# Input projection of an encoder layer: q and k of the first half side by side, in units of seven products

## The chip, the cores and the metric

One core of a Trainium2 chip runs the kernel. The metric is device microseconds from start to end of one execution; several executions are timed and their median is given. Engines are named as in the profile: PE is TensorE (PEld its weight loads), DVE is VectorE, ACT is ScalarE, POOL is GpSimd, SP is SyncE, which here only issues DMAs.

## The reference

One encoder layer on 256 tokens of width 2048, in float32:

```python
hn = rms_norm(h, g_mix_pre)
q, k, v, xr, yg = split(hn @ w_in, [1024, 2048, 3072, 4096])   # w_in: 2048 x 5120
attn = neighborhood_attention(q, k, v, rpb)                    # 8 heads of 128
rec = rglru_bidirectional(xr, ...) * gelu(yg)
h = h + rms_norm(concat(rms_norm(attn), rms_norm(rec)) @ w_out, g_mix_post)
fn = rms_norm(h, g_ffn_pre)
h = h + rms_norm((silu(fn @ w_ffn_gate) * (fn @ w_ffn_up)) @ w_ffn_down, g_ffn_post)
gate = sigmoid(rms_norm(h, g_ple_pre) @ w_ple_gate)
h = h + rms_norm(gate * (p @ w_ple_proj), g_ple_post)
```

The change is in the line with `w_in`.

## The kernel before

**Split products.** Each float32 operand is split into a high and a low part: ACT casts the high part (`wh`, line 700), DVE subtracts it from the operand for the low part (`wl`, line 716). A product of a block of activations with a block of weights is three matmuls with 512 columns, high by high, low by high, high by low (line 758), all added up in one PSUM bank. The activations (`hT_hi`, `hT_lo`, lines 331 and 333) are made from the transposed input `xs` in 16 blocks of 128 rows; they are the weights that PE loads, and the columns of `w_in` stream past them.

**Chunks and tiles.** The 5120 columns of `w_in` are ten chunks of 512, worked through in `ORDER`: x0 v0 q0 k0 x1 q1 k1 v1 g0 g1. A chunk has two PSUM banks, one for each 128 tokens. A weight tile holds two blocks of 128 rows (a pair: 0, 2, ... 14) of one chunk, 512 KB; with its two blocks and two halves of tokens it feeds four products, 12 matmuls. x0 and v0 take turns, tile by tile, but for their last two tiles (`turns(first, hT, KS, apart=2)`); every later chunk runs its eight tiles one after the other. The first three tiles are loaded and split by halves. When a chunk is done, its post (`xr_post`, `v_post`, `qk_post`, `yg_post`) evacuates the banks with the scale `rstd_x`, which `norm_x` gets from the rows of x (`xn`, four loads), and goes on beside the next chunks: transposes, gates, scans, heads.

**Units of seven.** Later stages (feed-forward, the last projection) already take some pairs as units: two chunks side by side, the two blocks of a pair and the two halves of the tokens form a 2 x 2 by 2 x 2 product, which a scheme of the Strassen and Winograd kind does with seven products instead of eight. A `Group` places the steps of its units: `four` (four products with sums of weights and of activations, `four_products`), `two` and `one` (the other three). Between them `made_of_four` recombines the four banks, once for all units of a group. The sums of activations come from `sums_of`, those of weights from `sum_stream`, and the last one adds a block of the second tile by an accumulating DMA from POOL's queue (`added`). The units need the two chunks' tiles of a pair with two blocks swapped, which `SWAPPED` does when the arrays are laid out.

**Who sets the order.** A planner (`Plan`) places every instruction when the program is built: streams of work (`load_stream`, `hi_stream`, `lo_stream`, `make_hT`, the posts) offer their next operation with a cost, and it takes the one that by its own clock can start first. What it writes is one fixed order for each engine, which the hardware follows; semaphores make an instruction wait for what it needs, and what stands behind it on its engine waits too. Weight tiles have four buffers (`wr`), freed by the low part made from them, and the next load on SP waits for that. High and low parts have four buffers each, freed by PE.

## Time and profile before

| | before |
|---|---|
| median of 3 runs | 1138.61 us (1137.95 to 1138.9) |
| the profiled execution | 1138.81 us |
| its span, first to last instruction | 1137.0 us |
| mean granted clock of PE | 0.998 |
| PE busy | 1127.5 us, 99% of the span |
| DVE busy | 962.1 us, 85% |
| ACT busy | 741.0 us, 65% |
| POOL busy | 154.5 us, 14% |
| chain that ended last | PE 96%, DVE 1%, ACT 1%, DMA 1% |
| moved by DMA | 269.54 MB, mean 237 GB/s |

The busy time of PE counts matmuls that overlap each other in its pipeline, so a share of 99% is not 99% of its peak; whether PE had holes is read from its waits and from the distance between the starts of matmuls. The other engines' shares are means over stages with different loads, so a stage is looked at by itself.

### The profile page before, as it was taken

The page shows a single profiled execution, that of the slowest core. Times are in us where ns is not written, and L with a number is a line of the kernel's source. Part 1 is how long each engine was busy: PE and PEld are TensorE (multiplying, and loading weights), DVE is VectorE, ACT ScalarE, POOL GpSimd, SP SyncE. Part 2 cuts the span into 40 slices and gives each one's busy share as a digit, 9 for nine tenths or more (in the row PEclk, how much of TensorE's full clock was granted, in tenths as well). Part 3 has the DMA queues.
Part 4 walks back from the last instruction along what each step waited for, and adds up shares of the span by engine and source line. Part 5 has one row for each costly group of instructions (what it writes and reads, how often), then busy time and mean ns, then how long its engine had stood idle before and what let it go on. Part 6 is the DMA issues. An engine that isn't in the chain of part 4 may idle for free.

```text
span 1137.0 us, 15223 instructions
## 1 busy us (share of the span) xinstructions
PE 1127.5 (99%) x5140; PEld 938.2 (83%) x5140; DVE 962.1 (85%) x1250; ACT 741.0 (65%) x994; POOL 154.5 (14%) x245
## 2 busy tenths in 40 slices
PE   9999999999999999999999999999999999999997
PEld 8888888888888888888888888888888888888886
DVE  6768787788469998899998889999989988888986
ACT  6776788876448566566566656666565664676674
POOL 0000000000000032232011043132121223200200
PEclk9999999999999999999999999999999999999999
DMA  8867566565686986887887777897887788967862
GB/s 311 303 193 219 173 183 187 166 201 181 206 302 184 344 254 226 234 259 222 277 285 232 240 222 216 249 269 235 271 275 280 233 242 255 305 208 271 269 198 101
DMA packets 110686, 269.54 MB, mean 237 GB/s; under 512 B 36432, under 2 KB 42576, under 8 KB 109200
## 3 DMA queue, kind: packets, MB, share of 16 engines
q1 hardware_dynamic: 95568, 242.60, 64.0%
q0 software_dynamic: 14752, 25.84, 11.1%
q8 instruction: 40, 0.66, 0.2%
q14 instruction: 38, 0.31, 0.1%
q10 hardware_dynamic: 288, 0.14, 0.0%
HBM read 250.70 MB, written 9.44 MB: 229 GB/s over the span
## 4 chain that ended last, share of the span: by engine, by line
PE 96%; DVE 1%; ACT 1%; DMA 1%; issue 0%; SPq 0%; DVEq 0%; POOL 0%; ACTq 0%; POOLq 0%
PE acc L758 69%; PE acc L769 8%; PE acc L768 8%; PE acc L767 8%; PE tr L344 1%; DVE wl L716 0%; DMA sq<-ev 0%; PE half L2119 0%; PE acc L2119 0%; PE warm L2305 0%; PE pg L391 0%; PE pg L392 0%; PE pg L393 0%; ACT wh L700 0%; PE po L1435 0%
## 5 line engine op out<-in xcount | busy, mean ns | idle before, releaser
L716 DVE TENSOR_TENSOR wl<-wr,wh 128x1024 fp32r<-128x1024 f32 (+1 forms) x295 | 352.9, 1210 | 77.8 <-ACT wh L700 72.4
L700 ACT CAST wh<-wr 128x1024 fp32r<-128x1024 f32 (+1 forms) x295 | 304.9, 1042 | 136.8 <-PE acc L758 84.2
L758 PE MATMUL acc<-wh,hT_mix_hi 128*128 128x512 f32 x376 | 146.6, 390 | 0.0
L758 PE MATMUL acc<-wh,hT_mix_lo 128*128 128x512 f32 x376 | 146.3, 389 | 0.0
L758 PE MATMUL acc<-wl,hT_mix_hi 128*128 128x512 f32 x376 | 146.3, 389 | 0.0
L700 ACT CAST wh<-ple 128x1024 fp32r<-128x1024 f32 (+1 forms) x75 | 76.0, 1018 | 82.2 <-DVE ple L643 54.6
L363 POOL DMA_DIRECT2D mT<-mid x164 | 96.8, 636 | 238.3 <-DVE mid L353 117.6
L758 PE MATMUL acc<-wl,hT_hi 128*128 128x512 f32 x320 | 124.6, 390 | 0.0
L758 PE MATMUL acc<-wh,hT_hi 128*128 128x512 f32 x316 | 124.5, 394 | 0.0
L758 PE MATMUL acc<-wh,hT_lo 128*128 128x512 f32 x316 | 123.2, 390 | 0.0
L669 POOL DMA_DIRECT2D ple<-in_w_ffn_up x32 | 28.7, 897 | 539.7 <-DVE ple L643 386.3
L716 DVE TENSOR_TENSOR wl<-ple,wh 128x1024 fp32r<-128x1024 f32 (+1 forms) x75 | 88.0, 1177 | 9.3 <-ACT wh L700 9.3
L758 PEld LDWEIGHTS acc<-wl,hT_mix_hi 128*128 128x128 f32 x376 | 70.6, 188 | 14.7 <-DVE wl L716 0.2
L758 PEld LDWEIGHTS acc<-wh,hT_mix_hi 128*128 128x128 f32 x376 | 70.6, 188 | 14.6
L758 PEld LDWEIGHTS acc<-wh,hT_mix_lo 128*128 128x128 f32 x376 | 70.6, 188 | 14.6
L758 PEld LDWEIGHTS acc<-wl,hT_hi 128*128 128x128 f32 x320 | 60.1, 188 | 13.1 <-DVE wl L716 0.2
L758 PEld LDWEIGHTS acc<-wh,hT_lo 128*128 128x128 f32 x316 | 59.4, 188 | 11.6
L758 PEld LDWEIGHTS acc<-wh,hT_hi 128*128 128x128 f32 x316 | 59.4, 188 | 11.4
L758 PE MATMUL acc<-w,hT_mix_hi 128*128 128x512 f32 x144 | 47.3, 389 | 0.0
L716 DVE TENSOR_TENSOR wl<-lower,wh 128x1024 fp32r<-128x1024 f32 x35 | 42.4, 1215 | 3.1 <-ACT wh L700 3.1
L700 ACT CAST wh<-lower 128x1024 fp32r<-128x1024 f32 x35 | 36.6, 1052 | 10.7 <-PE acc L758 6.8
L758 PE MATMUL acc<-wh,hT_ffn_hi 128*128 128x512 f32 x96 | 37.8, 393 | 0.4 <-ACT hT_ffn_hi L331 0.4
(472 smaller groups left out, 2536.6 us busy)
## 6 DMA issues: line engine op xcount, KB each, us to landing
wr<-in_w_in SPq DMA_DIRECT2D x77, 512.0 KB, 4.5
wr<-in_w_ffn_gate SPq DMA_DIRECT2D x70, 512.0 KB, 5.6
wr<-in_w_ffn_down SPq DMA_DIRECT2D x54, 512.0 KB, 6.0
wr<-in_w_ffn_up SPq DMA_DIRECT2D x50, 512.0 KB, 5.0
wr<-in_w_out SPq DMA_DIRECT2D x32, 512.0 KB, 4.4
wr<-in_w_ple_gate SPq DMA_DIRECT2D x30, 512.0 KB, 4.7
lower<-in_w_ffn_up SPq DMA_DIRECT2D x27, 512.0 KB, 6.4
third<-in_w_ffn_gate SPq DMA_DIRECT2D x18, 512.0 KB, 5.7
```

Source lines behind the costliest of these rows:

```text
L344: nc.tensor.transpose(tr[:, b, t * P : (t + 1) * P], e[:, t, sl], ident)
L363: (nc.gpsimd if i in pool else nc.sync).dma_start(dst[32 * j : 32 * j + 32, :, :, i, :], src[32 * i : 32 * i + 32, :, :, j, :],)
L669: nc.gpsimd.dma_start(dst, src, accum_op=ALU.add)
L700: nc.scalar.copy(his[i][:, 0 : src.shape[1], :] if n == 2 else his[i][:, j, :], src)
L716: nc.vector.tensor_tensor(out=los[i][:, m, :], in0=src, in1=f32(his[i][:, m, :]), op=ALU.subtract)
L758: nc.tensor.matmul(accs[t], x[:, sl], w[:, j, :], start=st and m == 0, stop=sp and m == 2, **group)
L767: nc.tensor.matmul(dst, x[0], wh, start=start, stop=False, skip_group_check=seeded)
L768: nc.tensor.matmul(dst, x[1], wh, start=False, stop=False, skip_group_check=seeded)
L769: nc.tensor.matmul(dst, x[0], wl, start=False, stop=stop, skip_group_check=seeded)
```

## The change

The first half's q and k become a `Group` with two units, the pairs 0 and 2 (`IN_KS`). Their `four` steps stand among the tiles of x0 and v0, both behind the fifth pair of those (`IN_AT`); x0 and v0 therefore use the banks of the kind `sm`, so that q0 and k0 can have the other four (`acc`) meanwhile. Behind x0 and v0 come q0's and k0's other pairs: 4, then the first unit's `two`, 6, then the second unit's `two` and both `one`, and then the last four tiles of q0 and the last four of k0. The second tile of a unit goes to a place of its own (`in_rows`, memory that q and k use later), and so do the sums (`in_both`, `here`). The loads of the rows of x move behind the units' loads. The pool of this stage is opened at the start, and tiles that share memory with the new ones are opened when chunks end.

```diff
+IN_KS = (0, 2)
+IN_AT = (5, 5)
...
+    (lambda c: (("w_in", c), ("w_in", c + 2)), (0,), IN_KS),
...
     def load_stream():
...
+            if i in in_load:
+                for kb, f in extra_loads.get((i, 0), ()):
+                    yield dma(kb)
+                    f()
+                j, second = in_load[i]
+                yield dma(512, take=None if second else "wr")
+                loaded[i] = in_rows[j] if second else raw_tile(i)
+                nc.sync.dma_start(loaded[i], a[w][n0 // N, k // 2])
+                done(ev_load[i])
+                continue
...
+    def in_sum_stream():
+
+        for j, i in enumerate(into.own):
+            yield ev_load[i]
+            yield ev_load[i + 1]
+            Q, R, both = loaded.pop(i), loaded.pop(i + 1), in_both[j]
+            yield dve(3 * N)
+            nc.vector.tensor_tensor(out=both[:, 0, :], in0=Q[:, 0, :], in1=Q[:, 1, :], op=ALU.add)
+            nc.vector.tensor_tensor(out=both[:, 1, :], in0=both[:, 0, :], in1=R[:, 1, :], op=ALU.add)
+            nc.vector.tensor_tensor(out=Q[:, 1, :], in0=Q[:, 1, :], in1=R[:, 1, :], op=ALU.add)
...
+    def in_last_sum(j):
+        late, last = into.last[j][:2]
+        there = Event()
+        yield from added(in_both[j][:, 1, :], late[:, 0, :], there)
...
+    def in_sums():
+        more = t1["pool"].tile([P, 2, N], F32R, name="sums_more")
+        pairs = [[x.rearrange("p k s -> p (k s)") for x in at0], (more[:, 0, :], more[:, 1, :])]
+        for n, kx in enumerate(IN_KS):
...
+            yield from sums_of(hT, kx, *p, t1["here"])
...
     for i in range(2 * NT):
-        extra_loads.setdefault((10 + i, 0), []).append(load_xn(i))
+        extra_loads.setdefault((14 + i, 0), []).append(load_xn(i))
...
-        ch = Chunk(post(half), (open_p1, second_tiles)[n] if n < 2 else None)
-        if n < 2:
-            first.append((ch, "w_in", n0 + half * N))
+        ch = Chunk(post(half), {0: open_hs, 1: open_v, 2: open_qk, 3: second_tiles}.get(n), slot="sm" if n < 2 else "acc")
+        made_of[c] = ch, "w_in", n0 + half * N
         if n == 1:
-            turns(first, hT, KS, apart=2)
-        elif n > 1:
-            seg(ch, "w_in", n0 + half * N, hT, KS, after=start_biases if n == 3 else None)
+            first = [made_of[m] for m in ORDER.split()[:2]]
+        if n == 3:
+            into = Group([made_of[m] for m in ORDER.split()[2:4]], hT, KS, IN_KS, apart=4)
+            into.own, into.twos, into.last = [], {}, {}
+            m = len(KS) - 2
+            for i, k in enumerate(KS[:m]):
+                for j, b in enumerate(IN_AT):
+                    if i == b:
+                        into.four(j)
+                for d, w, o in first:
+                    seg(d, w, o, hT, [k], i == 0, False)
...
+            for d, w, o in first:
+                seg(d, w, o, hT, KS[m:], first=False)
+            steps = list(('0', '1ab'))
+            m = len(into.rest) - into.apart
+            for i in range(m):
+                into.pair(i)
...
+            for d, w, o in into.chunks if into.apart else ():
+                seg(d, w, o, hT, into.rest[m:], first=False)
+        elif n > 3:
+            seg(*made_of[c], hT, KS)
...
+    plan.add(in_sums(), late=-LATE)
+    plan.add(in_sum_stream(), late=-LATE)
```

DVE at the start of the program, before. `wl_153` is the low part of x0's first tile (made by halves), `wl_166` that of v0's first tile, `wl_200` that of x0's second one, `hT0_lo` a block of the activations' low part:

```order
L716 TENSOR_TENSOR wl_153<-wr_137,wh_152 128x512
L716 TENSOR_TENSOR wl_166<-wr_141,wh_165 128x512 x2
L333 SCALAR_TENSOR_TENSOR hT0_lo_80<-xs0_81,g_first_67,hT0_hi_79 128x256 x2
L716 TENSOR_TENSOR wl_200<-wr_145,wh_199 128x512 x2
L716 TENSOR_TENSOR wl_214<-wr_149,wh_213 128x1024
```

The same place now. `wl_186` is x0's first tile, `wl_200` v0's first one, `wl_228` x0's second one, `here` the sums of activations:

```order
L927 TENSOR_TENSOR here_146<-hT0_hi_79,hT0_lo_80 128x256
L766 TENSOR_TENSOR wl_186<-wr_170,wh_185 128x512
L927 TENSOR_TENSOR here_146<-hT0_hi_79,hT0_lo_80 128x256
L766 TENSOR_TENSOR wl_200<-wr_174,wh_199 128x512
L336 SCALAR_TENSOR_TENSOR hT0_lo_80<-xs0_81,g_first_67,hT0_hi_79 128x256 x2
L934 TENSOR_TENSOR here_146<-here_146 128x128
L766 TENSOR_TENSOR wl_200<-wr_174,wh_199 128x512
L934 TENSOR_TENSOR here_146<-here_146 128x128
L766 TENSOR_TENSOR wl_228<-wr_178,wh_227 128x512
```

The two blocks of `hT0_lo` and an addition stand ahead of the second half of v0's first tile now; they stood behind it.

DVE some 20 us later, before. `wl_300` and `wl_322` are x0's and v0's fifth tiles (pair 8), the two behind them the sixth ones:

```order
L716 TENSOR_TENSOR wl_300<-wr_272,wh_299 128x1024
L333 SCALAR_TENSOR_TENSOR hT0_lo_80<-xs1_82,g_first_67,hT0_hi_79 128x256 x4
L716 TENSOR_TENSOR wl_322<-wr_285,wh_321 128x1024
L716 TENSOR_TENSOR wl_357<-wr_318,wh_356 128x1024
L716 TENSOR_TENSOR wl_377<-wr_354,wh_376 128x1024
```

The same place now. `wl_348` and `wl_387` are x0's and v0's fifth tiles, `wr_356` and `rows_qh` the two tiles of the first unit, `wr_384` and `rows_ql` those of the second, `both` the sums of weights, from which `wl_420` is made:

```order
L336 SCALAR_TENSOR_TENSOR hT0_lo_80<-xs1_82,g_first_67,hT0_hi_79 128x256 x2
L766 TENSOR_TENSOR wl_348<-wr_306,wh_347 128x1024
L336 SCALAR_TENSOR_TENSOR hT0_lo_80<-xs1_82,g_first_67,hT0_hi_79 128x256 x2
L330 TENSOR_TENSOR sums_more_148<-here_146,sums_more_148 128x512
L673 TENSOR_TENSOR both_kl_143<-wr_356 128x512
L674 TENSOR_TENSOR both_kl_143<-both_kl_143,rows_qh_140 128x512
L675 TENSOR_TENSOR wr_356<-wr_356,rows_qh_140 128x512
L766 TENSOR_TENSOR wl_387<-wr_324,wh_386 128x1024
L673 TENSOR_TENSOR both_pp_144<-wr_384 128x512
L674 TENSOR_TENSOR both_pp_144<-both_pp_144,rows_ql_141 128x512
L675 TENSOR_TENSOR wr_384<-wr_384,rows_ql_141 128x512
L766 TENSOR_TENSOR wl_420<-both_kl_143,wh_419 128x1024
```

Between the low parts of x0's and v0's fifth tiles stand a split and three additions of weights now, two of which read the unit's second tile.

SP at the loads of this place, before (`wr_285` is v0's fifth tile, `xs1` the last blocks of the transposed input, `xn` the rows of x):

```order
L612 DMA wr_285<-in_w_in 128x1024
L957 DMA xs1_82<-in_xT 128x1024
L965 DMA xn0_83<-in_x 128x1024
L612 DMA wr_318<-in_w_in 128x1024
L965 DMA xn0_83<-in_x 128x1024
```

and now (`wr_324` is v0's fifth tile):

```order
L626 DMA wr_324<-in_w_in 128x1024
L1015 DMA xs1_82<-in_xT 128x1024
L591 DMA wr_356<-in_w_in 128x1024
L591 DMA rows_qh_140<-in_w_in 128x1024
L591 DMA wr_384<-in_w_in 128x1024
L591 DMA rows_ql_141<-in_w_in 128x1024
L1023 DMA xn0_83<-in_x 128x1024
```

The four tiles of the units are issued where the rows of x were; up to there SP's order is the one of before.

## Rows read from the trace of the kernel before

**Rows 1.** The cores' spans and granted clock.
```profile
core 0: 1137.0 us, clock 0.998
```

**Rows 2.** Waits of PE, whole span: us in total, times, longest us.
```profile
PE final L2206 <- ACT diag L2204: 2.5, 1, 2.5
PE warm L2305 <- POOL ones L309: 1.1, 1, 1.1
PE acc L758 <- ACT hT_ffn_hi L331: 0.4, 1, 0.4
PE sc L391 <- DVE pp L327: 0.3, 1, 0.3
```

**Rows 3.** Chain of waits, one long piece: start us, us, what.
```profile
264.35 81.62 PE acc L758 x360
```

**Rows 4.** By stretches: PE, PEld, DVE, ACT, POOL busy us, PEclk, DMA share, GB/s.
```profile
10.00:20.00 10.00, 10.00 (x46) 8.13 (x45) 8.26 (x12) 6.92 (x11) 0.00 (x0) 1.00 0.98 370
20.00:30.00 10.00, 10.00 (x46) 8.29 (x45) 6.93 (x12) 7.74 (x13) 0.00 (x0) 1.00 0.96 344
30.00:40.00 10.00, 10.00 (x46) 8.29 (x45) 5.23 (x7) 8.67 (x13) 0.00 (x0) 1.00 0.93 349
...
90.00:100.00 10.00, 10.00 (x46) 8.27 (x45) 9.86 (x18) 5.73 (x8) 0.00 (x0) 1.00 0.69 194
```

**Rows 5.** Groups by line and shape, low and high parts of weights: busy us, mean ns.
```profile
L716 DVE TENSOR_TENSOR wl<-wr,wh 128x1024 fp32r<-128x1024 f32 x289 | 348.9, 1220 | 76.3 <-ACT wh L700 71.2 <-DMA wr<-in_w_in 1.8 <-PE acc L758 1.8
...
L700 ACT CAST wh<-wr 128x1024 fp32r<-128x1024 f32 x289 | 301.2, 1051 | 135.4 <-PE acc L758 84.2 <-PE acc L768 9.5 <-DMA wr<-in_w_in 6.2
```

**Rows 6.** Timeline from 5 to 12.5 us: start us, us, instruction [idle before <-releaser].
```profile
5.57 0.63 PE L743 MATMUL acc<-wh,hT_lo 128*128 128x512 f32 x1
...
6.00 0.60 PE L742 MATMUL acc<-wh,hT_hi 128*128 128x512 f32 x1
...
6.64 2.37 DVE L716 TENSOR_TENSOR wl<-wr,wh 128x512 fp32r<-128x512 f32 x3 [0.89 <-ACT wh L700]
...
9.30 0.91 ACT L331 ACTIVATE hT_hi<-xs,g_first 128x256 fp32r<-128x256 f32 x2 [1.02 <-DMA xs<-in_xT]
...
9.84 0.89 DVE L333 SCALAR_TENSOR_TENSOR hT_lo<-xs,g_first,hT_hi 128x256 fp32r<-128x256 f32 x2 [0.83 <-ACT hT_hi L331]
...
10.32 0.39 PE L758 MATMUL acc<-wl,hT_hi 128*128 128x512 f32 x1
...
10.75 1.29 DVE L716 TENSOR_TENSOR wl<-wr,wh 128x512 fp32r<-128x512 f32 x2
...
11.50 0.19 PEld L758 LDWEIGHTS acc<-wl,hT_hi 128*128 128x128 f32 x1
11.69 0.39 PE L758 MATMUL acc<-wl,hT_hi 128*128 128x512 f32 x1
```

**Rows 7.** Timeline of DVE near 18 and 363 us: instructions in a row.
```profile
17.72 2.35 DVE L716 TENSOR_TENSOR wl<-wr,wh 128x1024 fp32r<-128x1024 f32 x2
...
363.20 0.76 DVE L869 TENSOR_TENSOR ple<-hT_mix_hi,hT_mix_lo 128x256 f32<-128x256 f32 x2
364.00 1.02 DVE L876 TENSOR_TENSOR ple<-ple 128x128 f32<-128x128 f32 x4
```

**Rows 8.** Timeline of DVE from 24 to 28 us, its two waits for hT_hi.
```profile
24.20 0.89 DVE L333 SCALAR_TENSOR_TENSOR hT_lo<-xs,g_first,hT_hi 128x256 fp32r<-128x256 f32 x2 [0.98 <-ACT hT_hi L331]
...
26.49 1.69 DVE L333 SCALAR_TENSOR_TENSOR hT_lo<-xs,g_first,hT_hi 128x256 fp32r<-128x256 f32 x4 [0.27 <-ACT hT_hi L331]
```

**Rows 9.** DMA issues of the first 60 us: count, KB each, median us to landing.
```profile
wr<-in_w_in SPq DMA_DIRECT2D x21, 512.0 KB, 5.5
xn<-in_x SPq DMA_DIRECT2D x4, 512.0 KB, 10.0
```

**Rows 10.** By stretches at the end of the run, columns as in rows 4.
```profile
1128.00:1130.00 2.00, 0.70 (x5) 0.30 (x3) 1.15 (x4) 1.67 (x2) 0.00 (x0) 1.00 0.42 164
1130.00:1132.00 2.00, 0.70 (x2) 0.30 (x2) 1.50 (x5) 0.97 (x5) 0.00 (x0) 1.00 0.00 0
```

More of the change, by code (lines that the diff above doesn't have):

```diff
@@ L494, in two @@
             self.twos[j] = i
-            lower[self.own[j] + 1] = -1
+            if self.lhs is not hT:
+                lower[self.own[j] + 1] = -1
             segs.append((two_products, self, j, i))
@@ L650, in sum_stream @@
             done(ev_raw[two, 2])
+    def in_sum_stream():
[7 more added lines that the diff above has]
+            nc.vector.tensor_tensor(out=Q[:, 1, :], in0=Q[:, 1, :], in1=R[:, 1, :], op=ALU.add)
+            raws[i] = both
+            done(ev_raw[i, 2])
+            raws[i + 1], raws[into.twos[j]] = Q, R
+            done(ev_raw[i + 1, 2])
+            done(ev_raw[into.twos[j], 2])
+    def in_last_sum(j):
+        late, last = into.last[j][:2]
+        there = Event()
+        yield from added(in_both[j][:, 1, :], late[:, 0, :], there)
+        yield there
+        raws[last] = in_both[j][:, 1:2, :]
+        done(ev_raw[last, 2])
+    def in_sums():
+        more = t1["pool"].tile([P, 2, N], F32R, name="sums_more")
+        pairs = [[x.rearrange("p k s -> p (k s)") for x in at0], (more[:, 0, :], more[:, 1, :])]
+        for n, kx in enumerate(IN_KS):
+            if n == 2:
+                for e in hT.ev[8:]:
+                    yield e
+                pair = big(1, "sums_in").rearrange("p (n m) s -> p n (m s)", m=2)
+                pairs.append((pair[:, 0, :], pair[:, 1, :]))
+            p = pairs[n]
+            yield from sums_of(hT, kx, *p, t1["here"])
     ends_with, ends_in = {}, {}
@@ L726, in lo_stream @@
                 plan.add(last_sum(i), plan.now, -2 * SOON)
+            if i in into.own:
+                plan.add(in_last_sum(into.own.index(i)), plan.now)
     MM = 0.2263
@@ L811, in second @@
             done(there)
-        yield ev_rf
-        yield act(N)
-        u, v = (t2["pool"].tile([P, N], F32, tag="junk", name="u", bufs=2) for _ in range(2))
+        if group.lhs is hT:
+            u, v = (t1["ig"][:, n, :, :].rearrange("p c s -> p (c s)") for n in range(2))
+            yield act(N)
+        else:
+            yield ev_rf
+            yield act(N)
+            u, v = (t2["pool"].tile([P, N], F32, tag="junk", name="u", bufs=2) for _ in range(2))
         nc.scalar.copy(u, q1)
@@ L850, in one_product, with sums_of @@
         spent(i)
-    def sums_of(lhs, kx, hi, lo):
+    def sums_of(lhs, kx, hi, lo, here=None):
         lhs.sums[kx] = {
@@ L859, in sums_of @@
         yield lhs.ev[kx + 1]
-        kind = "mid" if lhs is hP or kx == 6 else "T4"
+        kind = None if here is not None else "mid" if lhs is hP or kx == 6 else "T4"
         for j in range(2):
@@ L863, in sums_of @@
             yield dve(S, take=None if j else kind)
-            if not j and kind == "mid":
+            if not j and not kind:
+                e, f = here[:, 0, :], here[:, 1, :]
+            elif not j and kind == "mid":
                 at_ = mid_tile()
@@ L1077, in open_p1, with open_v, open_qk, open_hs @@
         nc.gpsimd.memset(ssr, 0.0)
+        in_rows.extend(p1.tile([P, 2, N], F32, tag=n, name=f"rows_{n}") for n in ("qh", "ql", "kh"))
+        in_both.extend(p1.tile([P, 2, N], F32, tag=n, name=f"both_{n}") for n in ("kl",))
+        in_both.append(
+            p1.tile([P, 4 * NT * KEYS], F32, tag="pp", name="both_pp")[:, 0 : 2 * N].rearrange("p (m n) -> p m n", m=2)
+        )
+        in_both.append(sq_tile().rearrange("p t k q -> p t (k q)"))
+        t1["here"] = p1.tile([P, 2, N], F32, tag="vh", name="here")
+    def open_v():
+        for n in ("vh", "vl"):
+            t1[n] = t1["pool"].tile([P, NT, N], F32R, tag=n, name=n)
+    def open_qk():
+        for n in ("qh", "ql", "kh", "kl"):
+            t1[n] = t1["pool"].tile([P, HB, S], F32R, tag=n, name=n)
+        t1["pp"] = t1["pool"].tile([P, 2, NT, 2, KEYS], F32R, tag="pp", name="pp")
+    def open_hs():
+        t1["hs"] = big(0, "hs", F32)
     def sq_tile():
@@ L1100, in second_tiles @@
         plan.reach(ev_x)
+        t1["rec_hi"] = big(1, "rec_hi")
         t1["rec_lo"], t1["attnT"] = big(2, "rec_lo"), big(3, "attnT", F32)
@@ L2259, in layer @@
         places.append(lower[i])
+    in_load = {i + n: (j, n) for j, i in enumerate(into.own) for n in range(2)}
+    for i in in_load:
+        ev_load[i] = Event()
+    for j, i in enumerate(into.own):
+        gives[i] = gives[into.twos[j]] = gives[into.last[j][1]] = "x"
     first_slot = {i: n % 2 for n, i in enumerate(sorted(fours))}
@@ L2288, in layer @@
     soonest = min(fours)
+    open_p1()
     plan.add(load_stream(), late=lambda: (
```

19 lines of the change are left out of this document (12 added, 7 removed).

## The prediction

> **What bounds the kernel now.** I read the span first [rows 1], then TensorE's waits [rows 2]. Over the whole run it waited four times: 1.1 us before the first warm-up matmul, 2.5 us before the last matmul, 0.4 and 0.3 us between. The chain of waits gives the rate of the rest [rows 3]: 360 matmuls in 81.62 us, 0.2267 us each. So TensorE issues without a hole from the first weights on, and the time can move in two ways only: by the count of matmuls, and by new holes.
>
> Whether holes come is read where the change works, in the first 50 us. By stretches of 10 us [rows 4], VectorE is busy 8.26, 6.93 and 5.23 us from 10 us on, ScalarE 6.92 to 8.67, the DMA engines 98, 96 and 93%. That is some 9.6 us of idle VectorE in 30 us, and what it gets in addition has to fit in there at the right places, since an engine takes its instructions in the order in which they stand.
>
> **What it removes.** In two units q0 and k0 take seven products instead of eight: 2 x 1 x 3 matmuls of 512 columns fewer. 6 x 0.2267 = **1.36 us gained**. Nothing hides TensorE, so this counts in full, and it is all that can be gained.
>
> **What it adds.** VectorE gets 4 additions of 256 columns and 8 of 128 for the sums of activations, 2 low parts of 512 for those, 6 additions of 512 for the weights, 3 more low parts of 1024 (a unit casts three tiles and a half instead of two) and 4 additions of 512 that recombine the banks. At 0.38 and 0.26 us for 256 and 128 columns [rows 7], 0.65 for 512 [rows 6] and 1.22 for 1024 [rows 5] that is 1.5 + 2.1 + 1.3 + 3.9 + 3.7 + 2.6 = 15.1 us; the first four kinds (8.8 us) fall before the units. It is not free, and steps 1 and 2 price it. ScalarE gets 3 casts of 1024 at 1.05 us [rows 5], 2 of 512 and 2 copies, some 5.5 us: nothing as long as VectorE, which gets three times as much, is later; if it were ScalarE, the price is a cast, 1.05 us. The two accumulating loads of 256 KB go on GpSimd's queue, empty in this stage, and what they bring is used behind q0's and k0's next pairs and x0's and v0's last ones, some 25 us later: nothing. The four loads of x rows, moved on SP's queue behind the units' loads, serve only the scale with which x0 is evacuated, and that too moves back by the units' 5.4 us: nothing, or what x0's post is late, and TensorE doesn't wait for that before its transposes. These take the banks that x0 and v0 now hold; they stood 186 matmuls into the stage and stand 210 in now, and the 24 are the units' own: nothing. In the later stages TensorE's order is the same and buffers only rotate: nothing, as TensorE waited 0.4 us there [rows 2].
>
> **Step 1, a hole at 10 us.** Here the order decides. Before, the low part of v0's first pair, second half, was the third of three that ended at 6.64 + 2.37 = 9.01 us, and TensorE used it at 10.32 us [rows 6], 1.3 us later. Now the low part of hT of blocks 2 and 3 and one addition of 128 columns stand **ahead** of it. That hT_lo waits for ScalarE's hT_hi, which waits for a load until 9.30 us, so it starts at 9.84 us [rows 6], and the change leaves this load and ScalarE's order up to it as they were. So 9.84 + 0.41 + 0.41 (the row of two: 0.89 less the last one's tail) + 0.24 (128 columns) = 10.9 us, and 0.69 us for the low part (1.29 for two): 11.59 us. From there to TensorE: the next low part ended at 11.44 us (10.75 + 0.69), the weight load that waited for it began at 11.50 and its matmul at 11.69 [rows 6], 0.25 us. So TensorE goes on at 11.84 instead of 10.32: **1.5 us lost**. Bounds: 1.25 if the passage costs nothing; 1.8 if each small addition costs a wait as well.
>
> Behind this hole TensorE is 1.5 us late. The next five low parts are late by the small additions among them, and fit into that.
>
> **Step 2, the units' supply.** Next I set VectorE's work against TensorE's need, up to the low part of v0's fifth pair (v0/8), which now stands behind three weight additions. From 11.5 us VectorE has 12 hT_lo at 0.41, 2 additions of 256 at 0.38, 7 of 128 at 0.25, 7 operations of 512 at 0.61 and 7 low parts of 1024 at 1.13 us (spacings from [rows 6, 7]): 4.9 + 0.8 + 1.7 + 4.3 + 7.9 = 19.6, done at 31.1 us if it never waits. Before, it waited in this stretch 0.98 and 0.27 us for hT_hi [rows 8], which hangs on loads that don't come earlier now. I take the same 1.25 us: 32.35 us. TensorE asks, 90 matmuls after the hole, at 10.32 + 1.5 + 20.4 - 0.25 = 32.0 us: 0.35 us late. Then 3 additions and one low part (2.95 us) stand against 12 matmuls (2.72): 0.2 more. After that a tile of the units needs 1.13 us and lasts 1.36. **0.55 us lost.**
> Bounds: nothing, if VectorE waits 0.6 us less. Above, the units' second tiles decide. The first one is issued when x0/6's low part is done, about 24.1 us (54 matmuls after the hole), half a microsecond behind the first tile, and its addition stands at about 30 us. A load of weights took 5.5 us here in the median, one of x rows 10.0 [rows 9]. With 5.5 it lands as VectorE comes to it; with 10.0 everything behind waits 4.1 us longer.
>
> **Sum.** The profiled execution took 1138.81 us (its span 1137.0), 0.20 above the median of 1138.61. 1138.81 - 1.36 + 1.5 + 0.55 = 1139.5, on the scale of the median 1139.3. I say **1139.3 us**: the hole at 10 us eats the gain, the units' supply costs a little more. A measurement of this kernel can tell about 0.2% (2.3 us) from no change, so this counts as none.
>
> **Rivals.**
> A. *No hole*, the full gain: 1138.61 - 1.36 = 1137.25 us. For it: the idle time in [rows 4] suffices for the added work in sum. Against: step 1 hangs on one load at 9.30 us and the order behind it, not on the sum; that load would have to land 1.5 us earlier. 0.07.
> B. *The second tiles land late*, on the side of slower. Behind the addition that waits for them stand the low part of v0/8 and all that the units need. 0.7 us are lost by the forecast already (1139.3 less 1138.61), so another 1.6 us make more than 0.2%: it decides once such a tile takes more than 7.1 us instead of 5.5. For it: DMA engines 93 to 98% busy, and the 10.0 us of the x rows. Against: those rows now come later, so less is queued in front. 1139.8 to 1143.4 us. 0.20, half of it beyond 0.2%.
> C. *TensorE's clock falls in the hole.* The matmuls at 5.57 and 6.00 us start 0.43 us apart [rows 6], 1.2 GHz by their rate against 0.2267 us at 2.4 GHz, and TensorE had been at work since about 1 us. Some 5.3 us at half rate again would cost 2.65 us: 1141.9, slower. Against: before its last matmul TensorE stood for 2.5 us [rows 2], and the granted clock read 1.00 in both stretches around that [rows 10]. 0.04. The Trainium skill (TensorE: Matmul & The Clock Gate, Why this matters for your kernels) warns that idle gaps between bursts of matmuls bring the clock back to half; by this rule a change that opens a gap pays more than the gap, and the trace shows no such fall after its one long gap.
> D. *q0's post falls into VectorE's fullest stretch.* q0 ends 10.9 us ahead of k0 instead of 21.8, so its turn and splits move towards those of k0 and the first heads, and VectorE was busy 9.86 of 10 us from 90 to 100 us [rows 4]. A low part or two that come late there cost 1.13 us each: 1140.4 to 1141.6 us. 0.08.
>
> **How the numbers follow.** The forecast case has 0.61 and runs from 1138.4 (step 1 at its lower bound less a little, step 2 nothing) to 1140.3. The range 1137.9 to 1141.2 leaves out A, the upper third of B, C and a little of D, 0.2 in all. Slower by over 0.2% (above 1140.9): half of B, C, a third of D, 0.16. Faster by over 0.2% (below 1136.3): no term reaches it, since 1.36 us is all there is; 0.02 for what I don't see. The same: 0.82.
>
> **What would show it.** Step 1: a wait of TensorE (or of its weight load) for VectorE's low part at 10.3 us, some 1.5 us long, that low part ending near 11.6 us behind hT_lo at 9.84. Step 2: waits of under 1 us in all between 24 and 36 us, the first before v0/8. Elsewhere 0.2267 us between matmuls and six matmuls fewer. VectorE waiting long for rows_qh or rows_ql would show B, matmuls 0.43 us apart after 12 us C, TensorE waiting between 70 and 110 us D. I am wrong if TensorE has no wait at 10 us, or if its new waits sum to over 4 us.

## The result, and the profile after

The changed kernel took **1144.12 us** (median of 4 runs, 1142.26 to 1145.45) beside 1138.58 us of the kernel before in the same session (1137.95 to 1138.90): ratio 1.0047, 95% interval [1.0033, 1.0062]. It is slower by 5.5 us. The forecast was 1139.3 us, its range ended at 1141.2, and "slower by over 0.2%" had 0.16. The profiled execution took 1143.78 us, its span 1142.0 instead of 1137.0 [rows 1]; the differences below are told on the span.

TensorE's waits in the kernel after, over the whole span (us in total, times, longest us), with the same columns as [rows 2]:

```profile
PE acc L810 <- DVE wl L766: 3.1, 2, 1.7
PE final L2307 <- ACT diag L2305: 2.5, 1, 2.5
PE warm L2414 <- POOL ones L312: 1.1, 1, 1.1
PE tr L347 <- ACT pr L1456: 1.0, 1, 1.0
PE tr L347 <- ACT ev L1186: 0.5, 1, 0.5
PE acc L810 <- ACT hT_ffn_hi L334: 0.4, 1, 0.4
PE acc L794 <- ACT wh L750: 0.3, 1, 0.3
```

The waits of 2.5, 1.1 and 0.4 us are those of before. New are two for low parts (3.1 us), two of transposes (1.5 us) and one of 0.3 at the start. They sit in two places, the first 40 us and around 154 to 187 us. The first place by stretches, columns as in [rows 4]:

```profile
10.00:20.00 10.00, 8.60 (x38) 6.81 (x37) 9.36 (x18) 7.88 (x13) 0.00 (x0) 1.00 0.87 315
20.00:30.00 10.00, 8.31 (x37) 6.50 (x36) 7.73 (x16) 6.47 (x12) 0.00 (x0) 1.00 0.83 292
30.00:40.00 10.00, 9.88 (x44) 7.73 (x43) 9.86 (x14) 6.17 (x9) 0.99 (x1) 1.00 0.98 366
```

TensorE is no longer full. VectorE went from 8.26 to 9.36 us in the first stretch, where work was added. What was not forecast stands in the last two columns: the DMA engines fell from 98 and 96% to 87 and 83%, and from 370 and 344 to 315 and 292 GB/s. They moved less although there was more to load.

**The hole at 10 us** in the timelines of VectorE and TensorE (start us, us, instruction, idle before and its releaser):

```profile
10.22 0.89 DVE L336 SCALAR_TENSOR_TENSOR hT_lo<-xs,g_first,hT_hi 128x256 fp32r<-128x256 f32 x2 [1.37 <-ACT hT_hi L334]
11.02 0.28 DVE L934 TENSOR_TENSOR here<-here 128x128 f32<-128x128 f32 x1
11.22 0.69 DVE L766 TENSOR_TENSOR wl<-wr,wh 128x512 fp32r<-128x512 f32 x1
...
10.16 0.40 PE L810 MATMUL acc<-wh,hT_lo 128*128 128x512 f32 x1
11.96 0.50 PE L810 MATMUL acc<-wl,hT_hi 128*128 128x512 f32 x1 [1.40 <-DVE wl L766]
```

This is step 1, term by term: the two hT_lo, the addition of 128 columns, the low part. From 10.16 to 11.96 us, less one matmul of 0.23, are 1.57 us lost; 1.5 were forecast. Two small misses nearly cancel in that: the low part was done at 11.91 us instead of 11.59, as the load came later, and TensorE went on 0.05 us behind it instead of 0.25.

**The hole at 24 us** was in no step:

```profile
23.31 1.69 DVE L336 SCALAR_TENSOR_TENSOR hT_lo<-xs,g_first,hT_hi 128x256 fp32r<-128x256 f32 x4 [1.99 <-ACT hT_hi L334]
24.91 1.22 DVE L766 TENSOR_TENSOR wl<-wr,wh 128x1024 fp32r<-128x1024 f32 x1
...
24.11 0.39 PE L810 MATMUL acc<-wh,hT_lo 128*128 128x512 f32 x1
26.18 0.50 PE L810 MATMUL acc<-wl,hT_hi 128*128 128x512 f32 x1 [1.69 <-DVE wl L766]
```

The low part at 24.91 us is x0/6's. In the kernel before it is the second of the two in the row at 17.72 us [rows 7], ahead of the hT_lo of blocks 8 to 11, which begin there at 22.35 us:

```profile
22.35 0.87 DVE L333 SCALAR_TENSOR_TENSOR hT_lo<-xs,g_first,hT_hi 128x256 fp32r<-128x256 f32 x2
```

Now it stands behind these four hT_lo, which VectorE awaited for 1.99 us; x0/6's own high part was there at 19.25 us (the first row below). Why the four came late is read on ScalarE and on SP's queue (a row with x2 spans two issues and the wait between them):

```profile
18.20 1.05 ACT L750 CAST wh<-wr 128x1024 fp32r<-128x1024 f32 x1
22.77 1.71 ACT L334 ACTIVATE hT_hi<-xs,g_first 128x256 fp32r<-128x256 f32 x4 [0.83 <-DMA xs<-in_xT]
...
7.49 4.83 SPq L626 DMA_DIRECT2D wr<-in_w_in  x2
12.36 0.43 SPq L1015 DMA_DIRECT2D xs<-in_xT  x1
```

The second of the two wr is v0/4's load. It needs the buffer of v0's first tile, and so the very low part that is late at 10 us: it went out at 12 us, and the x blocks 6 and 7 behind it at 12.36 us (9.41 before). The next load, of x blocks 8 to 11, went out at 16.07 us (14.59 before). So one late low part cost TensorE 1.57 us at once and, by way of the loads queued behind it, most of 1.84 us at 24 us. The new order has a part in the second hole: ahead of the four hT_lo, x0/6's low part would not have waited for that load. This order was not tried by itself. There is one more hole in this part, 0.27 us at 37 us, at the units.

**The middle of the stage** (ScalarE, SP's queue, TensorE):

```profile
152.70 1.28 ACT L1456 ACT_TABLE_LOAD   x1 [1.57 <-DVE st L1451]
...
154.28 0.60 PE L347 MATMUL tr<-ident,ev 128*128 128x128 f32 x4
155.87 0.67 PE L347 MATMUL tr<-ident,pr 128*128 128x128 f32 x4 [0.99 <-ACT pr L1456]
...
180.36 1.93 SPq L366 DMA_DIRECT2D sq<-ev  x3
185.68 0.69 ACT L1186 ACTIVATE ev<-acc,rstd_x 128x512 f32<-128x512 f32 x1 [3.58 <-DMA sq<-ev]
...
187.52 0.55 PE L347 MATMUL tr<-ident,ev 128*128 128x128 f32 x3 [0.52 <-ACT ev L1186]
```

At 155.87 us the transposes of a head (pr) wait for ScalarE, 1.35 us against an unbroken row; ScalarE had stood 1.57 us for VectorE's st and then loaded a table for 1.28 us. At 187.52 us those of k1 wait for its evacuation, 0.73 us, which waited for the last of q1's turn (sq from ev) to leave the one buffer ev. ScalarE waited three times for this buffer between 100 and 200 us, 8.6 us in all; before twice, 2.8 us.

**The sum.** -1.36 (TensorE has 5134 matmuls instead of 5140) + 1.57 + 1.84 + 0.27 + 1.35 + 0.73 = +4.4. A wait of 0.5 us at 203 us in the kernel before is gone, which leaves 3.9 of the 5.0 us. The rest is one hole of 0.26 us at 255 us and many delays below 0.2 us, such as matmuls 0.233 instead of 0.227 us apart where a low part is only just there.

### The profile page after: what moved, and what is told of

Its sections match the earlier page's. It is cut to its first block, busy times and chain, and to the rows that moved or that the text cites. A ratio compares the mean times of both kernels' runs of the same rounds, so it can differ in the third digit from the quotient of the medians.

```text
span 1142.0 us, 15272 instructions
## 1 busy us (share of the span) xinstructions
PE 1127.6 (99%) x5134; PEld 935.6 (82%) x5134; DVE 974.8 (85%) x1278; ACT 742.7 (65%) x1000; POOL 156.3 (14%) x247
## 4 chain that ended last, share of the span: by engine, by line
PE 86%; DMA 5%; DVE 4%; ACT 3%; SPq 1%; issue 1%; DVEq 0%; ACTq 0%
PE acc L810 60%; PE acc L821 8%; PE acc L820 8%; PE acc L819 8%; DVE wl L766 1%; DMA wr<-in_w_in 1%; DMA xs<-in_xT 1%; DMA sq<-ev 1%; PE tr L347 1%; ACT wh L750 1%; DMA rows_ql<-in_w_in 1%; SPq L366 0%; DMA av<-in_w_rg_i 0%; PE half L2220 0%; PE acc L2220 0%
## 5 line engine op out<-in xcount | busy, mean ns | idle before, releaser
L810 PE MATMUL acc<-wh,hT_mix_hi 128*128 128x512 f32 x388 | 151.2, 390 | 0.0
L810 PE MATMUL acc<-wh,hT_mix_lo 128*128 128x512 f32 x388 | 151.0, 389 | 0.0
L810 PE MATMUL acc<-wl,hT_mix_hi 128*128 128x512 f32 x388 | 150.9, 389 | 0.0
L810 PE MATMUL acc<-wl,hT_hi 128*128 128x512 f32 x304 | 118.9, 392 | 3.2 <-DVE wl L766 3.1
L810 PE MATMUL acc<-wh,hT_hi 128*128 128x512 f32 x300 | 118.7, 396 | 0.0
L810 PE MATMUL acc<-wh,hT_lo 128*128 128x512 f32 x300 | 117.0, 390 | 0.0
L810 PEld LDWEIGHTS acc<-wl,hT_hi 128*128 128x128 f32 x304 | 57.0, 188 | 17.2 <-DVE wl L766 5.3
L810 PEld LDWEIGHTS acc<-wh,hT_lo 128*128 128x128 f32 x300 | 56.4, 188 | 10.9
L810 PEld LDWEIGHTS acc<-wh,hT_hi 128*128 128x128 f32 x300 | 56.4, 188 | 10.7 <-ACT wh L750 0.2
L810 PE MATMUL acc<-w,hT_mix_hi 128*128 128x512 f32 x120 | 39.4, 389 | 0.0
```

Source lines behind the costliest of these rows:

```text
L810: nc.tensor.matmul(accs[t], x[:, sl], w[:, j, :], start=st and m == 0, stop=sp and m == 2, **group)
```

## The experiments

All times are medians; the kernel before was measured beside each, at 1138.3 to 1138.7 us. "Holes" are start to start, less the matmuls between. Each profile is one execution, and not always a typical one.

### The load's buffer: is the hole at 24 us made by SP's queue?

```diff
     def raw_tile(i):
+        if i == OWN_RAW:
+            return t1["pool"].tile([P, 2, N], F32, tag="vl", name="own_raw")
...
     def raw_kind(i):
+        if i == OWN_RAW:
+            return None
...
+OWN_RAW = 5
```

> The changed kernel with every order as it is, but the sixth tile of weights (v0's third pair, v0/4) loaded into a buffer of its own, so that SP's queue does not wait there for the late low part of v0's first tile. Theory: the hole at 10 us stays as it is (1.4 to 1.6 us), but the loads behind that one are issued up to 3 us earlier, and the hole at 24 us (1.84 us) falls under 0.7; the time falls by 1.2 to 2 us. Rival (VectorE's own work makes the hole at 24 us, the late loads do not matter): it stays at 1.5 us or more and the time changes by less than 0.5 us.

**1141.55 us** (1140.62 to 1143.25), ratio 1.0027 [1.0015, 1.0038]: 2.6 us less than the changed kernel. SP's queue, VectorE and TensorE:

```profile
7.67 0.68 SPq L631 DMA_DIRECT2D own_raw<-in_w_in  x1
8.39 0.43 SPq L1020 DMA_DIRECT2D xs<-in_xT  x1
...
11.62 0.50 PE L815 MATMUL acc<-wl,hT_hi 128*128 128x512 f32 x1 [1.47 <-DVE wl L771]
...
31.32 1.22 DVE L771 TENSOR_TENSOR wl<-wr,wh 128x1024 fp32r<-128x1024 f32 x1
...
32.60 0.50 PE L815 MATMUL acc<-wl,hT_hi 128*128 128x512 f32 x1 [0.26 <-DVE wl L771]
```

The hole at 10 us is as before (1.63), the x blocks behind the load go out at 8.39 instead of 12.36 us, and the hole at 24 us is gone altogether. The theory holds, the rival falls. VectorE's order is unchanged, so loads that come in time are enough; that the order of before would do as well is not shown. What now remains up to 45 us is the forecast: v0/8's low part is done at 31.32 + 1.22 = 32.54 us (forecast 32.35), and TensorE loses 0.42 us there (forecast 0.35). This profile was the slowest of the seven runs: its span is only 0.6 us below that of the changed kernel, as a hole of 0.71 us at 109 us and one of 0.46 us at 476 us are new in it and the one at 185 us is 1.03 us.

### A second ev buffer: is the middle of the stage short of it?

```diff
-                e = t1["pool"].tile([P, NT, N], F32, tag="ev", name="ev")
+                e = t1["pool"].tile([P, NT, N], F32, tag="ev", name="ev", bufs=2)
```

On top of the own buffer; every order on every engine stays.

> The kernel with the sixth tile in a buffer of its own, every order as it is, and a second buffer for the evacuated chunks of the input projection (ev), so that an evacuation no longer waits until the turn of the chunk before it has left that buffer. Theory (the middle of the stage pays because q0's and k0's posts now follow each other closely and share this one buffer): ScalarE's waits for the turn's transfers at 111, 135 and 184 us (2.1, 2.9 and 3.8 us) go, the hole of the transposes at 185 us (1.03) goes, and the one at 153 us (0.99) at least halves; the time falls by 1.2 to 2 us from 1141.5 to about 1140. Rival (these holes come from the order alone, in which ScalarE and VectorE have too much ahead of the transposes): they stay within 0.4 us and so does the time.

**1140.25 us** (1138.96 to 1145.08, 12 runs), ratio 1.0020 [1.0011, 1.0028], 1.3 us less; the intervals of the two ratios overlap, so the times alone do not prove the step. In the profile the hole at 185 us is gone and the one at 151 us is 0.47 (0.3 is usual for a pair of transposes). The profiled execution happened to be the fastest run, and shows what the hole at 10 us hangs on. Its only wait of TensorE that the kernel before does not have, and its ScalarE:

```profile
PE acc L815 <- DVE wl L771: 0.2, 1, 0.2
...
8.37 0.91 ACT L339 ACTIVATE hT_hi<-xs,g_first 128x256 fp32r<-128x256 f32 x2
```

Here the load of x blocks 2 and 3 had landed by 8.37 us (9.67 in the changed kernel), and of the 1.57 us only 0.33 are lost.

### The sums of activations later

```diff
-    plan.add(in_sums(), late=-LATE)
+    plan.add(in_sums(), 16.0, late=-LATE)
```

> The changed kernel, with the sums of activations released to the order only from a planned time of 16 us on, so that VectorE's first twelve rows are those of the kernel before. Theory (the late low part at 10 us also holds SP's queue, so the loads behind it come late, and the hole at 24 us follows from that): no wait of TensorE for VectorE's low part at 10 us (1.57 us in the changed kernel), loads of x blocks 8 to 11 issued near 14.6 us instead of 16.1, the hole at 24 us gone, and holes of at most 1.2 us in all up to 45 us (my step 2, the supply of the units); the time falls by 2.5 to 3.5 us to about 1141. Rival (VectorE simply has too much work before the units): the hole at 10 us goes, but the time is lost again between 20 and 37 us, holes there of 2 us or more, and the time falls by less than 1.5 us.

**1158.34 us**, ratio 1.0178 [1.0162, 1.0193]. The hole at 10 us goes, but holes of 1.43, 0.81, 0.55, 1.56 and 0.49 us follow between 28 and 41 us and one of 1.16 us at 50 us: the rival's side, and the sums now come too late for the second unit. Most of the loss is elsewhere: the planner put everything behind it in another order, in which TensorE loses 3.2 us at 193 to 197 us and waits 6.4 us at 266 us, both for an evacuation (ev).

> The sums from 16 us on and the sixth tile in a buffer of its own, together. Theory: with the low parts in time nothing is held at that tile, so up to 45 us this is the kernel with the sums from 16 us on alone, within 0.5 us, and its time is the same within 0.8 us. Rival (there are too few buffers for weights in any case): holes up to 45 us smaller by another 0.5 us or more.

With the own buffer as well: **1156.97 us**. Against the theory the holes at 28 and 32 us went (2.2 us less): the buffers for weights are short even where that low part is in time. The 6.4 us at 265 us stayed.

### Side by side, without the units

```diff
-IN_KS = (0, 2)
-IN_AT = (5, 5)
+IN_KS = ()
+IN_AT = ()
...
-            steps = list(('0', '1ab'))
+            steps = []
```

> The changed kernel without the units: q0 and k0 run side by side behind x0 and v0, in the banks of the change, all with eight products, without sums of activations or weights; six matmuls more. Theory: no hole at 10, 24 and 37 us (under 0.4 us in all). For the waits of transposes at 154 and 187 us (2.1 us in the changed kernel) two theories: if they come from q0's and k0's posts lying closer together, they stay at 1 to 2 us and the time is 1139.6 to 1140.8; if they come from the units (their work and the order they shift), they go, and the time is that of the kernel before, 1138.6 within 0.5.

**1148.17 us**, ratio 1.0090 [1.0075, 1.0105]. No hole up to 60 us, as expected; after that some 8 us, in places where neither theory looked:

```profile
PE tr L347 <- ACT ev L1186: 1.9, 2, 1.1
PE pg L394 <- ACT xch L328: 1.7, 2, 1.4
PE acc L810 <- ACT ev L1186: 1.7, 1, 1.7
```

The granted clock falls here as well, to 0.50 at 105 to 108 us. So the middle of the stage can pay without any units: q0 and k0 side by side, in the order that the planner finds for that, cost more without them than with them. But that order is not the one with the units, so how much of the 2.08 us is theirs is not shown, nor which of the planner's choices does it.

### The planner told of the second ev buffer

Three runs, each with the own buffer and two ev buffers. In the first, `ev=1` among the planner's slots becomes `ev=2`. The second leaves that and takes the sums from 11 us on (`plan.add(in_sums(), 11.0, late=-2 * LATE)`). The third does both.

> As the one with two ev buffers, but the planner knows of the second one too, so that all orders from 90 us on may change. Theory (one buffer short): the planner puts evacuations earlier, no wait for the turn's transfers, and holes between 100 and 300 us of under 1 us in all; 1139.5 to 1140.5. Rival (each order that the planner finds has its own holes, in whatever place, since its durations are not the chip's): holes of 1.5 us or more in other places, 1141 or more.

**1143.09 us**, ratio 1.0038 [1.0024, 1.0053]; 2.8 us more than with the order kept. Holes of 1.71 us at 108 and 1.91 us at 147 us came in place of those at 151 and 185: the rival.

> The sums of activations from a planned time of 11 us on, ahead of everything else that is ready (behind the low parts of the first pairs, before those of x0's third), with the own buffer and two ev buffers. Theory: no hole at 10 us; the additions lie where VectorE waited for hT_hi, so the sums are there in time for the units and holes up to 45 us are under 1 us in all (1.6 and 0.4 in the kernel with the own buffer alone). Rival (VectorE cannot do all of this before the units in any order): the holes up to 45 us stay at 2 us or more in other places. What the middle of the stage costs in this order is open: without holes there it would be 1137.5, with those of the changed kernel 1139.5.

**1156.83 us**. The hole at 10 us goes and one of 3.62 us at 17 us comes: the additions, all in one place, delay the next low part. The rival, in a worse form. In the middle TensorE waits 6.3 us for ev once more.

> As the one with the sums from 11 us on, and the planner knows of the second ev buffer. Up to 45 us the same as that one within 0.3 us. In the middle of the stage, theory (one buffer short): holes under 1 us, 1137.5 to 1138.5, faster than before or equal to it; rival (each order has its own holes): 1.5 us or more there, 1139 or more.

**1145.92 us**, ratio 1.0065 [1.0052, 1.0078]. Told of the buffer, the planner loses nothing over 0.5 us behind 51 us, as the theory has it for the middle; the time misses its range by what comes before: a hole of 4.17 us at 17 us, with a granted clock of 0.50 for some 6 us from its end on, and one of 0.92 us at 49 us. That is 10.9 us less than the one before. The two rows of waits, of the one and of the other:

```profile
PE acc L815 <- ACT ev L1191: 6.3, 1, 6.3
```

```profile
PE acc L815 <- DVE wl L771: 4.8, 2, 4.0
```

### One exchange in VectorE's order

The plan is left as it is; only the two hT_lo of blocks 2 and 3 are issued behind the low part that they delayed.

```diff
-                yield from gained_split(
-                    hT_hi[:, b, :], hT_lo[:, b, :], xs[k][:, j, :], g_first[:, b : b + 1]
-                )
+                if b in BEHIND:
...
+                    nc.scalar.activation(hi, src, AF.Copy, scale=g)
+                    yield dve(S)
+                    behind.append((lo, src, g, hi))
...
+                while (i, j.stop) == (1, 2) and behind:
+                    lo, x, g, hi = behind.pop(0)
+                    nc.vector.scalar_tensor_tensor(
...
```

> The changed kernel with one exchange in VectorE's order and nothing else: the low part of v0's first tile, second half, stands ahead of the two hT_lo of blocks 2 and 3. No buffers added. Theory (the hole at 10 us is that order and that load, and the one at 24 us follows from it): both go (1.57 and 1.84 us; up to 0.5 us may remain at 10 to 12 us, as the two hT_lo now stand ahead of the next low part), SP's queue issues x blocks 6 and 7 near 9.4 us instead of 12.4, and some 0.5 us stay between 30 and 37 us; the waits at 154 and 187 us stay (2.1 us): 1140.5 to 1141.2. Rival (the loads are late for another reason): only the hole at 10 us goes, 1142.5.

**1144.81 us** (1142.59 to 1145.94), no gain, against the theory. The holes at 10 and 24 us did go, and x blocks 6 and 7 go out at 9.92 us. In their place stand 0.92 us at 5.9 us (a load of weights lands later than in the changed kernel, where 0.49 us are lost there), 0.69 us at 14.8 us, 1.60 us at 32.4 us (the load of x blocks 12 to 15 lands at 27 us, VectorE waits 2.04 us for it) and 2.03 us at 111 us; the waits at 154 and 187 us shrank to 0.2, with the one buffer ev: TensorE comes to the second 2.3 us later than in the changed kernel, and ScalarE 1.9. What TensorE gained early it lost at the next thing that was only just in time. Behind the hole at 111 us something else shows, in TensorE's timeline and by stretches (columns as in [rows 4]):

```profile
113.10 0.50 PE L817 MATMUL acc<-wl,hT_hi 128*128 128x512 f32 x1 [1.87 <-DVE wl L768]
113.83 0.63 PE L817 MATMUL acc<-wh,hT_lo 128*128 128x512 f32 x1
114.25 0.63 PE L817 MATMUL acc<-wl,hT_hi 128*128 128x512 f32 x1
...
114.00:115.00 1.00, 1.00 (x5) 0.81 (x4) 0.78 (x1) 0.67 (x2) 0.00 (x0) 0.50 0.86 127
117.00:118.00 1.00, 1.00 (x7) 0.84 (x6) 1.00 (x3) 0.57 (x1) 0.00 (x0) 1.00 0.56 229
```

The granted clock falls to 0.50, which is 1.2 GHz, for some 3 us after a wait of 1.87 us; the matmuls start 0.42 us apart. At half rate, 3.3 us cost some 1.5 us more (an estimate from the distances of the starts, 0.42 instead of 0.23 and 0.21 instead of 0.12 us). This is rival C of the prediction, in another place.

> The same exchange, with the buffer of its own for the sixth tile and two ev buffers. Theory: the three causes of the loss are gone together, holes under 0.8 us in all, and the 1.36 us of the six matmuls show: 1137.2 to 1138.2, faster than before by up to 0.1%, and scattering less than the one without the exchange (1138.96 to 1145.08). Rival (something else that the trace has not shown costs as well): 1138.5 or more.

**1140.43 us** (1137.90 to 1144.25, 11 runs), ratio 1.0022 [1.0010, 1.0033]. The rival: no better than without the exchange. The hole at 10 us is now one of 0.67 us at 14 us, one of 0.55 stands at 107 us, and one of 0.7 us is back at 183 us in spite of the second ev buffer. There the second half of k1's evacuation stands on ScalarE behind a cast that reads q1's turn (sq), and this cast waits for the turn's last transfers:

```profile
182.44 0.62 ACT L335 CAST qh<-sq 128x512 fp32r<-128x512 f32 x1 [3.53 <-DMA sq<-ev]
```

Three of the runs, at 1143.7 to 1144.25 us, read a mean granted clock of 0.996; the other eight 0.998 or 0.999. 0.002 of 1140 us are 2.3 us, of some 4 us that part them.

> The exchange and the two ev buffers, without the buffer of its own for the sixth tile. Theory (that buffer only mattered because the low part was late): the same as with it, within 0.5 us. Rival (buffers for weights are short in any case): a hole of 0.5 us or more between 20 and 40 us, and 0.5 to 1 us more time.

**1142.75 us** (1140.96 to 1148.43), ratio 1.0043 [1.0025, 1.0062]. The rival: a hole of 1.61 us at 31 us is back. The own buffer matters beyond the late low part.

### The hole at 107 to 111 us

In the run with the exchange alone, SP's queue, ScalarE and VectorE:

```profile
98.07 4.95 SPq L368 DMA_DIRECT2D sq<-ev  x6
104.05 0.38 SPq L1229 DMA_DIRECT2D av<-in_w_rg_a  x1
...
109.60 1.05 ACT L330 CAST gh<-av 128x1024 fp32r<-128x1024 f32 x1 [3.12 <-DMA av<-in_w_rg_i]
110.68 1.23 DVE L332 TENSOR_TENSOR gl<-av,gh 128x1024 fp32r<-128x1024 f32 x1 [3.22 <-ACT gh L330]
```

The loads of the gates' weights (av) stand behind the transfers of q0's turn, and the low part that TensorE wants is the row after gl. So the loads go to GpSimd's queue:

```diff
-                nc.sync.dma_start(
+                nc.gpsimd.dma_start(
                     raw[:, 4 * z + 2 * i : 4 * z + 2 * i + 2, :],
```

> The kernel with the exchange, the own buffer and two ev buffers, and the loads of the gates' weights (av) issued on GpSimd's queue instead of SP's; every other order as it is. Theory (at 107 to 111 us VectorE's gl, and the low part behind it, waits for these loads, which stand behind the turn's transfers on SP's queue): that hole goes, the runs near 1144 us with a granted clock of 0.996 go, and the median falls from 1140.4 to 1138.0 to 1139.2. Rival (the hole has another cause, such as the work of VectorE and ScalarE there): it stays at 0.4 us or more, and the median within 0.6 us.

**1139.67 us** (1138.96 to 1140.78, 11 runs), ratio 1.0007 [0.9998, 1.0016], the best version. The hole is gone (gl runs at 105.20 us without a wait), no run shows a clock under 0.997, and the scatter is 1.8 instead of 6.4 us. The theory holds; the median is half a microsecond over its upper end. The edit moves the first half's loads as well, from 55.0 to 37.5 us, and a hole of 0.75 us at 54 us, at the transposes of x0, is new in this run and the two below; whether these loads make it was not tried.

> The same, and every second of the turn's small transfers (sq from ev) on GpSimd's queue as well. Theory (SP's queue, in which loads of weights wait behind transfers that wait, is what the middle of the stage hangs on): the waits of the transposes at 151 and 183 us (0.5 and 0.7 us) go too, 1137.2 to 1138.2, faster than the kernel before by 0.1% or equal to it. Rival (GpSimd's queue issues more slowly and the turn ends later): holes of 1 us or more after 110 us, 1139 or more.

Every second transfer of the turn on GpSimd's queue too (`if i in pool or take == "sq" and i % 2`): **1139.76 us**, ratio 1.0010 [1.0001, 1.0019], nothing more. The waits at 151 and 183 us were already gone in the version before it, where ScalarE's cast of sq waits 1.00 us instead of 3.53; so theory and rival are not told apart.

> The version with the gates' weights on GpSimd's queue, with one more exchange: hT_hi of block 4 behind the cast of v0/2 on ScalarE and hT_lo of block 4 behind its low part on VectorE; every other order as it is. Theory (the same cause as at 10 us: work that waits for a load stands ahead of a low part whose weights are there): the hole at 14.3 us (0.69) goes without another in its place, and the median falls by 0.5 to 0.8 us to 1138.9 to 1139.2, no difference to the kernel before. Rival (the load of block 4 sets the next matmuls in any order): the hole moves to 15.6 us, to x0/4, and the time stays within 0.3 us.

hT_hi and hT_lo of block 4 behind v0/2's cast and low part, by the same means: **1139.80 us**, ratio 1.0013 [1.0004, 1.0022]. The hole of 0.69 us at 14.3 us goes and one of 0.78 us at 17.1 us comes: the rival, one tile further on. In the first 18 us it is the loads that are short, and an exchange only chooses who waits.

So the best version cannot be told from the kernel before. Its span of 1137.8 us beside 1137.0 is: -1.36 for the matmuls, +0.69 at 14 us, +0.75 at 54 us (transposes of x0), +1.0 in delays under 0.2 us, -0.5 for a wait of the kernel before at 203 us that is gone: +0.6 of 0.8 us.

## Why the prediction was wrong

**The gain** was right: six matmuls fewer, 1.36 us. **Step 1** was right in mechanism: 1.57 us against 1.5, with VectorE's rows in the order told. That the size fits so closely is in part luck, since a load 0.3 us later and a passage 0.2 us shorter made up for each other, and in the fastest profile, where that load landed earlier, the hole was 0.33 us.

**The sentence behind step 1 failed**, and with it a term of step 2. "The next five low parts are late by the small additions among them, and fit into that", and "I take the same 1.25 us" for VectorE's waits for hT_hi, took it that a low part which is late delays TensorE alone. It also gives back a buffer, and SP's queue, which issues in order, stood some 4 us before the load that wanted this buffer, with the x blocks behind it; what stands queued behind the late one was asked for VectorE and not for SP. The fifth of these low parts, x0/6's, was moreover put behind four hT_lo that wait for such a load; the sum counted them for v0/8 and did not ask where in the row they stand. VectorE's waits for hT_hi from 11.5 to 31 us were 2.4 us, 1.99 of them right ahead of x0/6's low part: a term of 1.84 us that the sum did not have. The 1.25 us were also misread: in that stretch VectorE waited a third time for hT_hi in the kernel before, 0.81 us ahead of the row

```profile
15.39 0.49 DVE L333 SCALAR_TENSOR_TENSOR hT_lo<-xs,g_first,hT_hi 128x256 fp32r<-128x256 f32 x1 [0.81 <-ACT hT_hi L331]
```

The run with the own buffer shows it alone: with SP's queue freed at that one load the hole is gone, and step 2 measures 0.42 us at the low part that it named (0.35 forecast there, 0.55 with the units); VectorE's waits in that stretch sum to 1.22 us there, which is near the 1.25 by luck. The Trainium skill (DMA: Bandwidth & Descriptors, Anatomy of one DMA — SWDGE (gpsimd) path) says, where it describes transfers that GpSimd issues, that the DMA engines do not wait for semaphores and that any such wait is spent on the issuing sequencer, before dispatch; SP's queue shows the same, with some 4 us between its two issues in the row at 7.49 us.

**"In the later stages TensorE's order is the same and buffers only rotate: nothing" failed.** The planner puts the whole middle of the stage in another order: between 50 and 200 us the rows of TensorE, VectorE, ScalarE and SP's queue stand in other places in the two traces. Rival D had the thought (posts that collide) but placed it at 70 to 110 us, priced it by low parts of VectorE, and gave it 0.08. What came was at 154 and 187 us, 2.08 us. Behind the second hole stand the last transfers of q1's turn, which ScalarE awaits for 3.58 us. In the changed kernel it does so for the one buffer ev; with a second one and the same order the hole is gone from the profile. But the buffer is one way of two: with two of them ScalarE still awaits these transfers with its cast of sq, 2.62 us in that profile, and with the exchange as well it is 3.53 us, and 0.7 us are lost. For the first hole, only that it shrank with the second buffer (1.35 in the changed kernel, 0.99 with the own buffer, 0.47 with both) is shown. Why these 2.08 us come with this order stays open beyond that.

**The rivals.** A (no hole) did not come; that it "hangs on one load" did: where that load landed by 8.37 us the hole was 0.33. B (second tiles late) did not come: the additions waited 0.1 us at most for rows_qh and rows_ql in the changed kernel. C did not come in the changed kernel: the granted clock reads 1.00 after 1.40 and after 1.69 us of waiting. It did come in variants. Besides the one at 111 us above, it fell during a wait of 6.36 us with the sums from 16 us on (the first two rows, by stretches), and without the units after waits of 1.41 and 0.34 us (the last two, a matmul and a stretch):

```profile
270.00:273.00 3.00, 0.00 (x0) 0.00 (x0) 3.00 (x6) 2.97 (x6) 0.00 (x0) 0.50 0.26 52
273.00:276.00 3.00, 3.00 (x8) 2.31 (x9) 2.74 (x4) 1.32 (x3) 0.00 (x0) 0.50 0.67 205
...
103.49 0.38 PE L394 MATMUL pg<-xch,gh 128*128 128x256 f32 x1 [1.41 <-ACT xch L328]
...
106.00:107.00 1.00, 1.00 (x4) 0.81 (x4) 1.00 (x2) 0.99 (x2) 0.00 (x0) 0.50 0.87 139
```

The prediction set against C that the clock read 1.00 around the wait of 2.5 us before the last matmul. Its rows end at 1132 us [rows 10]; from 1132.8 us on the same trace reads 0.50:

```profile
1133.00:1135.00 2.00, 0.00 (x0) 0.00 (x0) 0.18 (x1) 0.00 (x0) 0.00 (x0) 0.50 1.04 367
```

TensorE had started its last matmul at 1131.49 us, so nothing was left to be slowed; but a trace that shows this fall does not speak against C. The prediction read it as one without a fall, against the rule in the Trainium skill (TensorE: Matmul & The Clock Gate, Why this matters for your kernels) that idle gaps between bursts of matmuls bring the clock back to half. The variants do show such falls, after gaps as short as these, and there a gap costs more than itself.

**Its own signs.** The prediction called itself wrong if TensorE's new waits summed to over 4 us. They sum to 4.9 us by the list of waits above, 3.1 in the first 40 us for low parts, 1.5 at transposes and 0.3 at the start.

**In sum:** the terms that were in it measured near the forecast, -1.36 + 1.57 + 0.42 (the last with the own buffer; in the changed kernel 0.27, at the units). Two were missing: 1.84 us (SP's queue held by the late buffer, and x0/6's place behind that load), and 2.08 us in the middle of the stage (another order, with ScalarE behind the turn's transfers).

## What to carry to other kernels

When an instruction becomes late, ask what it gives back as well as what it delivers: a buffer that comes free late holds the load that wants it, and on a queue in order everything behind that load. Where a planner sets the order, a change at the start of a stage is a change of all of it, and an order that was measured good is lost: the same units cost from 1139.7 to 1158.3 us here, by order, buffers and queues alone. And where TensorE is only just supplied, a hole that is taken away becomes time gained only if the next thing that is just in time has room; the exchange took away two holes and gained nothing.

## What the runs showed of the hardware

The load of x blocks 2 and 3 (256 KB) was issued at 3.54 to 3.56 us in all sixteen profiles, with the same loads ahead of it. ScalarE began the cast that reads it between 8.37 and 9.73 us, in twelve of them straight from a wait for it: over a microsecond of spread, which this change turned into a hole and which the kernel before did not feel.

The granted clock did not tell all of the start. In the kernel before it reads 1.00 where matmuls start 0.43 us apart [rows 6]:

```profile
5.00:6.00 1.00, 1.00 (x4) 0.81 (x4) 0.75 (x2) 0.19 (x2) 0.00 (x0) 1.00 0.93 315
```

In the changed kernel's profile the matmuls of this place start 0.23 us apart. Later the clock did show falls to 0.50: during waits of TensorE of 4.01 and 6.36 us, and behind waits of 3.46, of 1.87, of 2.05 and 0.77, of 1.67 and 0.77, and of 1.41 and 0.34 us. It did not fall behind single waits of 1.40 and 1.69 us (the changed kernel), 1.72 us (without the units), 1.74 us (the planner told of ev) and 1.91 us (the sums from 11 us on). So the length of one wait did not tell whether it fell. Behind the 2.5 us before the last matmuls it fell 1.7 us later, when no matmul was left.
